# Attention of five of six head pairs in tied runs on TensorE

## Chip, cores and metric

The program runs on one core of one Trainium2 chip. The metric is the device time of one execution in microseconds, as a median over runs.

## What is computed

Two layers of a causal decoder, on a prompt of 1024 tokens and 8 single tokens with caches. The change lies in the prompt's attention. There are three groups of four heads of 64 channels; group g has window and dilation (128, 1), (512, 4), (2048, 16). A query reads the keys at distances 0, d, 2d, ... up to its window. The reference, cut to this:

```python
sc = jnp.einsum('brnqhd,brnkhd->brnhqk', qs, ks) * ATT_SCALE      # blocks of 128 queries, keys of the block before and its own
sc = jnp.where(mask[None, None, :, None], sc, NEG_INF)
m = jnp.max(sc, axis=-1, keepdims=True)
p = jnp.exp(sc - m)
l = jnp.sum(p, axis=-1, keepdims=True)
o = jnp.einsum('brnhqk,brnkhd->brnqhd', p, vs) / jnp.moveaxis(l, 3, 4)
...
att = jnp.sum(wts[..., None] * jnp.stack(outs, axis=0), axis=0)   # merge of the three groups
cv  = swish(layer_norm(causal_depthwise_conv31(a * sigmoid(gate))))
x   = x + concat(att, cv) @ w_o
x   = x + relu(rms_norm(x) @ w_up)**2 @ w_down
```

## The kernel before

Activations lie with channels on partitions, 1032 tokens along the free axis. All of it is fp32; the large products split both factors into a high and a low fp32r part and add three matmuls (lines 217 to 219, `ws_job`).

A layer's first half is a list of units, `STEPS` (line 60). `('g', j)` computes one 128-channel tile of the GLU (tile `gluL`) and sets off its convolution, 46 taps on VectorE (line 413). `('v', g)` and `('qk', g, p)` project v, and q and k of two heads, into `zv` and `zk`; then TensorE turns them by transposes (`tv`, `tz`, `tq`, `tk`). `('at', g, p)` is the attention of head pair p of group g, the function `attend`. `('ln',)` normalises the convolution's outputs, `('mg', p)` merges the groups for a head pair, and the products with w_o follow (`woL`).

`attend` works on eight tiles of 128 queries. A tile has one block of 128 keys (all of group 2, the even tiles of group 1, the first of group 0) or two. For two tiles at a time:
- scores, S: per tile and head one matmul (line 609) into the PSUM banks `sc`, one per head. Its operands have 64 rows, half of the array. The trace shows two matmul records for each fp32 matmul, so S of two tiles are eight.
- softmax: VectorE adds the mask and takes the extremum (line 618, into tile `sm`); ScalarE takes the exponential and its sum (line 621).
- turning, T: one transpose on TensorE per head and key block (line 628), into a bank `tr`, which ScalarE copies to `pT` (line 630). One record each.
- product with v, V: per head and key block one matmul (line 634) into the bank `pv`, with 64 columns of the array. Two records each: 4 per tile with one block, 8 with two.

In the program text T, the copy and V of the first tile precede T, the copy and V of the second; the next two tiles' S come after both. After four tiles ScalarE copies the bank `pv` to the output `O`.

There are two buffers each of `sc`, `tr`, `sm`, `pT`, one of `pv`, nine of `v` and three of `qT`. `sc` and `tr` are shared with the turnings of the q, k and v units.

Nothing in the program text fixes the order on an engine. A planner does it when the program is built: among the instructions whose inputs and buffers are ready by its own account of time it takes the one traced first (`later` and `next_piece` shift that place; the convolution's taps are traced 1300 places later). Each engine then runs its list strictly in that order. `tc.issue_after(ins)` adds one constraint: what is traced inside it comes behind `ins` in the list of the same engine; other instructions may still come in between.

So TensorE's list mixes large products of the units to come with the S, T and V of the attention at hand.

Of the kernel before, what the change touches and what calls it, by code (L numbers as in the profile page):

```python
# [7 lines left out]
F32 = mybir.dt.float32  # L8
F32R = mybir.dt.float32r
AF = mybir.ActivationFunctionType  # L10
ALU = mybir.AluOpType
# [4 lines left out]
P = 128  # L16
# [6 lines left out]
HD = 64  # L23
# [52 lines left out]
def tile_hybrid_decoder_step(  # L76
# [20 lines left out]
    nc = tc.nc  # L97
# [42 lines left out]
    def ps_s(name):  # L140
        return state["ps"].tile([P, 2, 256], F32, tag="sc", name=name, bufs=2)

    def ps_t(name):
        return state["ps"].tile([P, 4, P], F32, tag="tr", name=name, bufs=2)

    def ps_o(name):
        return state["ps"].tile([P, 4, P], F32, tag="pv", name=name, bufs=1)
# [74 lines left out]
    for l in range(DEPTH):  # L222
        for b in range(NB):
            for kv in range(2):
                for g, (win, _) in enumerate(GROUPS):
                    n = (win - 1) * 256
# [5 lines left out]
                    for q in range(parts):  # L232
                        o = q * rows * step
# [4 lines left out]
    def prow(l, what, j):  # L238
        base = {"mix": 0, "ffn": 8, "cb": 16, "lg": 22, "lb": 28}[what]
        return prm[:, NC_L * l + base + j:NC_L * l + base + j + 1]  # L240
# [4 lines left out]
    def act(k, name):  # L245

        return tp.tile([P, TOK], F32, tag="act", name=name, bufs=NCT) if k < NCT else big(name)

    def spare(name):

        return tp.tile([P, TOK], F32, tag="out", name=name, bufs=2)
# [93 lines left out]
    def by_group(t, g):  # L345

        if g == 0:
            return t
        if g == 1:
            return t.rearrange("p (i q) -> p q i", q=4)  # L350
        return t.rearrange("p (c r) -> p r c", r=16)

    def layer(l, x_dram, xin, last):
        nm = f"L{l}"
        xh, xl, rstd, norm_rest = xin
        with ExitStack() as pa:
            ap_ = pa.enter_context(tc.tile_pool(name=f"A{l}", bufs=1, reuse_waits="tile"))
# [17 lines left out]
            mask = ap_.tile([P, 256], F32, tag="mask", name=f"mask{nm}")  # L375
            mask2 = ap_.tile([P, P], F32, tag="mask2", name=f"mask2{nm}")
# [7 lines left out]
            vt = {}  # L384
            stat = {}
# [206 lines left out]
            def attend(g, p, qT, kT):  # L592
                if g not in stat:
                    stat[g] = ap_.tile([P, 8, 8], F32, tag="stat", name=f"stat{nm}_{g}", bufs=2)
                o_t = spare(f"O{nm}_{g}{p}")
                O = o_t[:, 0:SEQ]
                for half in range(2):
                    po = ps_o(f"po{nm}_{g}{p}{half}")
                    for n0 in range(4 * half, 4 * half + 4, 2):
                        tiles = []  # L600

                        sh = [ps_s(f"s{nm}_{g}{p}{n0}{h}") for h in range(2)]
                        for i in range(2):
                            n = n0 + i
                            blocks = (n - 1, n) if (g == 0 and n > 0) or (g == 1 and n % 2 == 1) else (n,)
                            tiles.append((n, blocks, P * len(blocks)))
                            for h in range(2):
                                hs = slice(HD * h, HD * h + HD)
                                nc.tensor.matmul(sh[h][:, i, :P * len(blocks)], qT[half][hs, n - 4 * half, :],  # L609
                                                 kT[hs, blocks[0]:n + 1, :].rearrange("p b t -> p (b t)"), start=True, stop=True)  # L610
                        sms = []
                        for i, (n, blocks, w) in enumerate(tiles):
                            sm = ap_.tile([P, 2, 256], F32, tag="sm", name=f"sm{nm}_{g}{p}{n}", bufs=2)
                            sms.append(sm)
                            mk = mask2 if g == 2 else (mask if len(blocks) == 2 else mask[:, P:256])
                            for h in range(2):
                                c = 2 * p + h
                                nc.vector.tensor_tensor_reduce(  # L618
                                    out=sm[:, h, :w], in0=sh[h][:, i, :w], in1=mk, scale=1.0, scalar=3.0e38,
                                    op0=ALU.add, op1=ALU.min, accum_out=stat[g][:, n, c:c + 1])  # L620
                                nc.scalar.activation(sm[:, h, :w], sm[:, h, :w], AF.Exp, bias=stat[g][:, n, c:c + 1], scale=-1.0,  # L621
                                                     accum_out=stat[g][:, n, 4 + c:5 + c])
                        for sm, (n, blocks, w) in zip(sms, tiles):
                            pt = ps_t(f"pt{nm}_{g}{p}{n}")
                            nbk = len(blocks)
                            for h in range(2):
                                for b in range(nbk):
                                    nc.tensor.transpose(pt[:, nbk * h + b, :], sm[:, h, P * b:P * b + P], ident)
                            pT = ap_.tile([P, 4, P], F32, tag="pT", name=f"pT{nm}_{g}{p}{n}", bufs=2)
                            nc.scalar.activation(pT[:, :2 * nbk, :], pt[:, :2 * nbk, :], AF.Copy)  # L630
                            for h in range(2):
                                for b in range(nbk):
                                    v = vt[g][blocks[b]]
                                    nc.tensor.matmul(po[HD * h:HD * h + HD, n - 4 * half, :],  # L634
                                                     v[:, P * p + HD * h:P * p + HD * h + HD],
                                                     pT[:, nbk * h + b, :], start=(b == 0), stop=(b == nbk - 1))
                    if g == 0:
                        nc.scalar.activation(O[:, 512 * half:512 * half + 512], po.rearrange("p n t -> p (n t)"), AF.Copy)
                    elif g == 1:
                        nc.scalar.activation(O.rearrange("p (b i q) -> p q b i", b=2, q=4)[:, 2 * half:2 * half + 2],  # L640
                                             po.rearrange("p (q b) i -> p q b i", q=2), AF.Copy)
                    else:
                        nc.scalar.activation(by_group(O, 2)[:, 8 * half:8 * half + 8],
                                             po.rearrange("p n (r c) -> p (n r) c", r=2), AF.Copy)
                if g > 0:
                    od = dp.tile([P, SEQ], F32, tag=f"od{g}{p}", name=f"od{nm}_{g}{p}", bufs=1)
                    nc.gpsimd.dma_start(od, O)
                    odram[g, p] = od
                else:
                    att[p] = o_t  # L650
# [170 lines left out]
            for what, *at in STEPS:  # L821
# [6 lines left out]
                elif what == "qk":  # L828
                    g, p = at
# [5 lines left out]
                elif what == "at":  # L835
                    g, p = at
# [8 lines left out]
                elif what == "sv":  # L845
                    values = sample_values(*sample_softmax())
# [56 lines left out]
        with ExitStack() as pb:  # L903
# [8 lines left out]
            def parts_of(op, name):  # L912

                out = []
                for i in range(2):
                    if op in ("t3", "b11", "t2", "t1", "b12"):
                        hl = [xs.tile([P, TOK], F32R, tag=t, name=f"{op}{t}{name}{i}", bufs=8) for t in ("xh", "xl")]
                    else:
                        hl = [bp.tile([P, TOK], F32R, tag=t, name=f"{op}{t}{name}{i}", bufs=6) for t in ("oh", "ol")]
                    out.append(tuple(t.rearrange("p (k t) -> p k t", k=2) for t in hl))  # L920
                return out
# [165 lines left out]
            o = ops["t2"] = parts_of("t2", f"U{nm}")  # L1087
# [97 lines left out]
            for g in range(1, NG):  # L1185
                c = {}
# [38 lines left out]
            for k in range(KD):  # L1225
                t = act(k, f"y{nm}_{k}")
                nc.scalar.dma_start(t, x_scr[:, k, :])
                y.append(t)
            for c in range(NG // 2):
                ops.clear()  # L1230
                for _, op in PRODUCTS:
                    o = ops[op] = parts_of(op, f"D{nm}_{c}")
                    for i in range(2):
                        h, lo_t = o[i]
# [137 lines left out]
    h, lo, acc, sq = norm_split(first, lambda k: prow(0, "mix", k), "m0", True)  # L1372

    ident = const.tile([P, P], F32, name="ident")
# [21 lines left out]
    for l in range(DEPTH):  # L1396
        src = (lambda k: xT[:, k, :]) if l == 0 else (lambda k: x_scr[:, k, :])
        last = Last(l)
# [105 lines left out]
```

## Time and profile before

| | |
|---|---|
| median of 3 runs | 2533.15 us (2531.63 to 2537.89) |
| profiled execution, its time | 2538.58 us |
| its span | 2536.8 us |
| mean granted clock of TensorE | 0.993 |
| instructions | 47393 |
| TensorE matmul, weight load | 2476.8 us (98%), 2337.9 us (92%) |
| VectorE, ScalarE, GpSimd | 1882.1 us (74%), 1081.1 us (43%), 240.3 us (9%) |

Busy time is the time in which an engine has at least one instruction in flight. TensorE's matmuls overlap, so the sum of their lengths is more than its busy time, and what a matmul costs is read from the distance of starts. An instruction's row has its line of the kernel, its output and inputs by the program's names, and its shape; for TensorE first the part of the array that it uses (128\*128 all of it, 64\*128 half of the rows, 128\*64 half of the columns). A row can stand for several instructions of one kind that follow each other.

### The profile page before, as it was taken

The numbers are of one execution on the slowest core, as the hardware profiler recorded it, in microseconds if no ns is written. First come the engines' busy times: TensorE is split into PE (matmuls) and PEld (weight loads), VectorE is DVE, ScalarE is ACT, GpSimd is POOL, SyncE is SP. The second block draws the span as 40 slices with busy tenths as digits, with TensorE's granted clock in tenths as the row PEclk, the third lists the DMA queues.
The fourth block names the chain that finished last, engine by engine and source line by source line (L and its number), as shares of the span: only waits on it lengthen the run. The fifth ranks groups of instructions, "written<-read, shape, count | busy, mean of one in ns | idle before, by whom it ended". The sixth has DMA issues, their size and how long they took to land. (4 is left out here: it accounts for less than half of the span.)

```text
span 2536.8 us, 47393 instructions
## 1 busy us (share of the span) xinstructions
PE 2476.8 (98%) x18872; PEld 2337.9 (92%) x18872; DVE 1882.1 (74%) x3308; ACT 1081.1 (43%) x2044; POOL 240.3 (9%) x445
## 2 busy tenths in 40 slices
PE   8999999998999999999999999999989999999997
PEld 7988988888999999999999888878989999999996
DVE  7988886677756687777778788766677756876776
ACT  5244447544433353334423443484444333543332
POOL 1001101011101021001010020010101101111000
PEclk9999999999999999999999999999999999999999
DMA  5324323353455587455333242243425555955451
GB/s 175 115 75 116 117 73 120 128 175 123 156 195 188 179 319 250 154 177 206 115 105 109 83 128 76 89 134 134 167 88 203 197 187 199 335 194 199 144 180 68
DMA packets 153390, 391.62 MB, mean 154 GB/s; under 512 B 32256, under 2 KB 54384, under 8 KB 150608
## 3 DMA queue, kind: packets, MB, share of 16 engines
q1 hardware_dynamic: 91072, 210.72, 25.5%
q0 software_dynamic: 43904, 147.95, 16.9%
q10 hardware_dynamic: 18192, 29.91, 3.5%
q8 instruction: 148, 2.42, 0.4%
q14 instruction: 74, 0.61, 0.1%
HBM read 299.38 MB, written 177.06 MB: 188 GB/s over the span
## 5 line engine op out<-in xcount | busy, mean ns | idle before, releaser
L217 PE MATMUL gluL<-xhm,whi 128*128 128x384 f32 (+2 forms) x592 | 188.6, 323 | 10.3 <-ACT whi L198 5.7
L219 PE MATMUL gluL<-xhm,wlo 128*128 128x384 f32 (+2 forms) x592 | 188.8, 321 | 0.0
L218 PE MATMUL gluL<-xlm,whi 128*128 128x384 f32 (+2 forms) x592 | 188.4, 320 | 0.4 <-DVE xlm L262 0.4
L217 PE MATMUL zkL<-xhm,whi 128*128 128x264 f32 (+2 forms) x576 | 187.4, 326 | 1.1 <-ACT zkL L476 1.1
L218 PE MATMUL zkL<-xlm,whi 128*128 128x256 f32 (+2 forms) x576 | 187.9, 326 | 0.0
L219 PE MATMUL zkL<-xhm,wlo 128*128 128x264 f32 (+2 forms) x576 | 186.5, 325 | 0.0
L199 DVE TENSOR_TENSOR wlo<-raw,whi 128x512 fp32r<-128x512 f32 x156 | 106.3, 687 | 40.9 <-ACT whi L198 39.0
L413 DVE SCALAR_TENSOR_TENSOR cL<-uL,cwt,cL 128x512 f32<-128x512 f32 x180 | 133.8, 743 | 0.3 <-ACT cL L411 0.3
L413 DVE SCALAR_TENSOR_TENSOR cL<-bxL,hsum,cL 128x512 f32<-128x512 f32 x180 | 133.8, 743 | 0.1
L198 ACT ACTIVATE whi<-raw 128x512 fp32r<-128x512 f32 x156 | 96.5, 632 | 82.2 <-DMA raw<-in_dram 44.9
L413 DVE SCALAR_TENSOR_TENSOR bxL<-uL,cwt,bxL 128x512 f32<-128x512 f32 x168 | 125.2, 745 | 0.0
L217 PEld LDWEIGHTS gluL<-xhm,whi 128*128 128x128 f32 x592 | 111.5, 189 | 13.3 <-ACT whi L198 5.7
L217 PEld LDWEIGHTS zkL<-xhm,whi 128*128 128x128 f32 x576 | 108.4, 188 | 13.1 <-issue 3.7
L219 PEld LDWEIGHTS zkL<-xhm,wlo 128*128 128x128 f32 x576 | 108.7, 189 | 12.8 <-issue 5.2
L218 PEld LDWEIGHTS zkL<-xlm,whi 128*128 128x128 f32 x576 | 108.5, 188 | 12.4 <-issue 4.9
L218 PEld LDWEIGHTS gluL<-xlm,whi 128*128 128x128 f32 x592 | 111.8, 189 | 2.2 <-DVE xlm L262 1.3
L219 PEld LDWEIGHTS gluL<-xhm,wlo 128*128 128x128 f32 x592 | 111.7, 189 | 2.1 <-issue 1.2
L1244 DVE TENSOR_TENSOR yL<-yL,paDL 128x516 f32<-128x516 f32 x128 | 87.3, 686 | 27.9 <-PE paDL L1156 27.9
L621 ACT ACTIVATE smL<-smL,statL 128x128 f32<-128x128 f32 (+1 forms) x192 | 84.6, 443 | 35.0 <-DVE statL L618 34.0
L217 PE MATMUL zvL<-xhm,whi 128*128 128x512 f32 (+2 forms) x288 | 95.5, 332 | 1.1 <-ACT zvL L473 0.8
L219 PE MATMUL zvL<-xhm,wlo 128*128 128x512 f32 (+2 forms) x288 | 93.2, 325 | 0.0
L218 PE MATMUL zvL<-xlm,whi 128*128 128x512 f32 (+2 forms) x288 | 93.0, 323 | 0.0
(525 smaller groups left out, 9235.2 us busy)
## 6 DMA issues: line engine op xcount, KB each, us to landing
raw<-in_dram SPq DMA_DIRECT2D x408, 256.0 KB
out_kvs_dram<-in_dram SPq DMA_DIRECT2D x128, 511.8 KB
out_kvs_dram<-in_dram SPq DMA_DIRECT2D x32, 511.0 KB
x_scr<-xL POOLq DMA_DIRECT2D x32, 258.0 KB, 3.5
fdL<-f11L POOLq DMA_DIRECT2D x16, 516.0 KB, 3.1
fdL<-f21L POOLq DMA_DIRECT2D x16, 516.0 KB, 5.0
fdL<-f22L POOLq DMA_DIRECT2D x16, 516.0 KB, 3.1
fdL<-t3fL POOLq DMA_DIRECT2D x16, 516.0 KB, 3.6
```

Of the source, the lines that this page charges most:

```text
L198: nc.scalar.activation(hi, raw, AF.Copy)
L199: nc.vector.tensor_tensor(lo, raw, hi.bitcast(F32), op=ALU.subtract)
L217: nc.tensor.matmul(out[:, :n], a, h, start=(k == 0), stop=False)
L218: nc.tensor.matmul(out[:, :n], a, l, start=False, stop=False)
L219: nc.tensor.matmul(out[:, :n], b, h, start=False, stop=(k == nk - 1))
L413: nc.vector.scalar_tensor_tensor(dst, src(m), tap(m), dst, op0=ALU.mult, op1=ALU.add)
L621: nc.scalar.activation(sm[:, h, :w], sm[:, h, :w], AF.Exp, bias=stat[g][:, n, c:c + 1], scale=-1.0, accum_out=stat[g][:, n, 4 + c:5 + c])
L1244: nc.vector.tensor_tensor(o, o, p, op=ALU.add)
```

## The change

`attend` is cut into four functions: `scores` (S and softmax of two tiles), `turn` (T of two tiles, last tile and last head first, and the copies to `pT`), `values` (V of two tiles) and `end` (the copy of the bank `pv`). The loop runs `turn` of the tiles at hand, then `values` of the two tiles before them, then `scores` of the next two. For all head pairs but (0, 1), TensorE's instructions are put behind one another by `issue_after`: the first T of a step stands behind the last S, every other T behind that first one, V behind the last T, the next S behind the last V. For (0, 1) there is no such tie, and `values` takes the tiles just turned.

```diff
+                po, last = {}, []
+                together = (g, p) != (0, 1)
+                def behind():
+                    return tc.issue_after(last[-1].ins) if last and together else nullcontext()
+                def scores(n0):
...
+                    with behind():
+                        for i in range(2):
...
+                                mm = nc.tensor.matmul(sh[h][:, i, :P * len(blocks)], qT[half][hs, n - 4 * half, :],
+                                                      kT[hs, blocks[0]:n + 1, :].rearrange("p b t -> p (b t)"), start=True, stop=True)
+                    last.append(mm)
...
+                def turn(tiles):
+                    pts = [ps_t(f"pt{nm}_{g}{p}{n}") for _, n, _ in tiles]
+                    for pt, (sm, n, blocks) in reversed(list(zip(pts, tiles))):
+                        nbk = len(blocks)
+                        for h in (1, 0):
+                            for b in range(nbk):
+                                with behind():
+                                    mm = nc.tensor.transpose(pt[:, nbk * h + b, :], sm[:, h, P * b:P * b + P], ident)
+                                if n == tiles[-1][1] and h == 1 and b == 0:
+                                    last.append(mm)
+                    last.append(mm)
...
+                def values(tiles):
+                    for pT, n, blocks in tiles:
+                        half, nbk = n // 4, len(blocks)
+                        if half not in po:
+                            po[half] = ps_o(f"po{nm}_{g}{p}{half}")
+                        for h in range(2):
+                            for b in range(nbk):
+                                v = vt[g][blocks[b]]
+                                with behind():
+                                    mm = nc.tensor.matmul(po[half][HD * h:HD * h + HD, n - 4 * half, :],
+                                                          v[:, P * p + HD * h:P * p + HD * h + HD],
+                                                          pT[:, nbk * h + b, :], start=(b == 0), stop=(b == nbk - 1))
+                    last.append(mm)
+                    n = tiles[-1][1]
+                    if n % 4 == 3:
+                        end(n // 4)
...
+                sm, pT = scores(0), None
+                for n0 in range(0, 8, 2):
+                    turned = turn(sm)
+                    if pT:
+                        values(pT)
+                    pT = turned
+                    if not together:
+                        values(pT)
+                        pT = None
+                    if n0 < 6:
+                        sm = scores(n0 + 2)
+                if pT:
+                    values(pT)
```

## Rows read from the trace of the kernel before

**Rows 1.** The page, engines: busy us, share of the span, instructions.

```profile
PE 2476.8 (98%) x18872; PEld 2337.9 (92%) x18872; DVE 1882.1 (74%) x3308; ACT 1081.1 (43%) x2044; POOL 240.3 (9%) x445
```

**Rows 2.** Stretches: length, busy PE, PEld, DVE, ACT, POOL, clock, DMA; layer 2's sum.

```profile
160.60:195.70 35.10, 35.10 (x236) 30.37 (x236) 21.47 (x65) 17.52 (x57) 0.22 (x2) 1.00 0.24 72
216.30:260.00 43.70, 40.99 (x294) 36.34 (x294) 37.31 (x90) 20.27 (x61) 9.82 (x15) 1.00 0.46 105
310.40:355.20 44.80, 44.80 (x286) 34.59 (x284) 39.86 (x86) 23.33 (x65) 1.49 (x2) 1.00 0.30 90
394.10:476.00 81.90, 81.90 (x597) 66.46 (x595) 49.95 (x137) 65.62 (x154) 10.14 (x18) 1.00 0.43 142
...
sum 206.40, PE 203.32 PEld 167.67 DVE 149.53 ACT 126.79 POOL 21.65; mean PE 50.83 PEld 41.92 DVE 37.38 ACT 31.70 POOL 5.41
```

**Rows 3.** Groups of instructions by shape, TensorE, 160.6 to 195.7 us.

```profile
L217 PE MATMUL gluL<-xhm,whi 128*128 128x384 f32 x32 | 11.1, 346 | 0.0
...
L217 PE MATMUL gluL<-xhm,whi 128*128 128x264 f32 x14 | 4.1, 289 | 0.0
```

**Rows 4.** Order of time, TensorE, around four V: start us, us, instruction.

```profile
175.32 0.28 PE L217 MATMUL gluL<-xhm,whi 128*128 128x264 f32 x1
175.53 0.44 PE L634 MATMUL poL<-pTL,vL 128*64 128x128 f32 x4
175.90 0.39 PE L218 MATMUL gluL<-xlm,whi 128*128 128x264 f32 x1
176.13 0.28 PE L219 MATMUL gluL<-xhm,wlo 128*128 128x264 f32 x1
```

**Rows 5.** Order of time, TensorE, around two T.

```profile
172.34 0.38 PE L628 MATMUL ptL<-ident,smL 128*128 128x128 f32 x2
172.47 0.37 PE L217 MATMUL gluL<-xhm,whi 128*128 128x264 f32 x1
172.68 0.28 PE L218 MATMUL gluL<-xlm,whi 128*128 128x264 f32 x1
172.80 0.28 PE L219 MATMUL gluL<-xhm,wlo 128*128 128x264 f32 x1
```

**Rows 6.** Order of time, TensorE, V, T and S in one run.

```profile
410.67 0.93 PE L634 MATMUL poL<-pTL,vL 128*64 128x128 f32 x12
411.53 0.44 PE L628 MATMUL ptL<-ident,smL 128*128 128x128 f32 x2
411.90 0.93 PE L609 MATMUL sL<-kTL,qTL 64*128 64x128 f32 x8
412.75 0.50 PE L218 MATMUL zkL<-xlm,whi 128*128 128x512 f32 x1
```

**Rows 7.** Order of time, TensorE, around eight S.

```profile
160.41 0.28 PE L219 MATMUL zkL<-xhm,wlo 128*128 128x264 f32 x1
160.62 0.72 PE L609 MATMUL sL<-kTL,qTL 64*128 64x128 f32 x8
161.27 0.44 PE L217 MATMUL gluL<-xhm,whi 128*128 128x384 f32 x1
161.55 0.33 PE L218 MATMUL gluL<-xlm,whi 128*128 128x384 f32 x1
161.72 0.34 PE L219 MATMUL gluL<-xhm,wlo 128*128 128x384 f32 x1
```

**Rows 8.** Order of time, first reduction and last exponential of two tiles.

```profile
220.49 0.29 DVE L618 CUSTOM_DVE_ANT_0 smL<-sL,mask2L 128x128 f32<-128x128 f32 x1
...
221.99 0.39 ACT L621 ACTIVATE smL<-smL,statL 128x128 f32<-128x128 f32 x1
```

**Rows 9.** Waits of TensorE, whole run: us in total, times, longest us.

```profile
PE poL L634 <- ACT pTL L630: 1.9, 2, 1.1
```

**Rows 10.** Waits of VectorE, 160 to 560 us.

```profile
DVE smL L618 <- PE sL L609: 12.3, 7, 6.1
```

**Rows 11.** Instructions on tile clL to 640 us: ns min/median/max, first and last start.

```profile
L860 DVE TENSOR_TENSOR clL<-cL,chL x6: 1217/1222/1231, 450.0 to 460.0; 128x1024 fp32r<-128x1024 f32 x6
```

More of the change, by code (lines that the diff above doesn't have):

```diff
@@ L596, in attend @@
                 O = o_t[:, 0:SEQ]
[L597 to L602, printed above, removed]
+                po, last = {}, []
[3 more added lines that the diff above has]
+                def scores(n0):
+                    half = n0 // 4
+                    tiles = []
+                    sh = [ps_s(f"s{nm}_{g}{p}{n0}{h}") for h in range(2)]
+                    with behind():
                         for i in range(2):
@@ L608, in attend @@
                                 hs = slice(HD * h, HD * h + HD)
[L609 to L636, printed above, removed]
+                                mm = nc.tensor.matmul(sh[h][:, i, :P * len(blocks)], qT[half][hs, n - 4 * half, :],
+                                                      kT[hs, blocks[0]:n + 1, :].rearrange("p b t -> p (b t)"), start=True, stop=True)
@@ new lines, in scores @@
+                    last.append(mm)
+                    out = []
+                    for i, (n, blocks, w) in enumerate(tiles):
+                        sm = ap_.tile([P, 2, 256], F32, tag="sm", name=f"sm{nm}_{g}{p}{n}", bufs=2)
+                        out.append((sm, n, blocks))
+                        mk = mask2 if g == 2 else (mask if len(blocks) == 2 else mask[:, P:256])
+                        for h in range(2):
+                            c = 2 * p + h
+                            nc.vector.tensor_tensor_reduce(
+                                out=sm[:, h, :w], in0=sh[h][:, i, :w], in1=mk, scale=1.0, scalar=3.0e38,
+                                op0=ALU.add, op1=ALU.min, accum_out=stat[g][:, n, c:c + 1])
+                            nc.scalar.activation(sm[:, h, :w], sm[:, h, :w], AF.Exp, bias=stat[g][:, n, c:c + 1], scale=-1.0,
+                                                 accum_out=stat[g][:, n, 4 + c:5 + c])
@@ new lines, in scores @@
+                    return out
+                def turn(tiles):
[9 more added lines that the diff above has]
+                    last.append(mm)
+                    out = []
+                    for pt, (sm, n, blocks) in reversed(list(zip(pts, tiles))):
+                        nbk = len(blocks)
+                        pT = ap_.tile([P, 4, P], F32, tag="pT", name=f"pT{nm}_{g}{p}{n}", bufs=2)
+                        out.append((pT, n, blocks))
+                        nc.scalar.activation(pT[:, :2 * nbk, :], pt[:, :2 * nbk, :], AF.Copy)
+                    return out[::-1]
@@ new lines, in values @@
+                def values(tiles):
[3 more added lines that the diff above has]
+                            po[half] = ps_o(f"po{nm}_{g}{p}{half}")
+                        for h in range(2):
+                            for b in range(nbk):
[8 more added lines that the diff above has]
+                        end(n // 4)
@@ L637, in attend, with end @@
+                def end(half):
+                    o = po[half]
                     if g == 0:
-                        nc.scalar.activation(O[:, 512 * half:512 * half + 512], po.rearrange("p n t -> p (n t)"), AF.Copy)
+                        nc.scalar.activation(O[:, 512 * half:512 * half + 512], o.rearrange("p n t -> p (n t)"), AF.Copy)
                     elif g == 1:
                         nc.scalar.activation(O.rearrange("p (b i q) -> p q b i", b=2, q=4)[:, 2 * half:2 * half + 2],
-                                             po.rearrange("p (q b) i -> p q b i", q=2), AF.Copy)
+                                             o.rearrange("p (q b) i -> p q b i", q=2), AF.Copy)
@@ L642, in attend @@
                     else:
                         nc.scalar.activation(by_group(O, 2)[:, 8 * half:8 * half + 8],
-                                             po.rearrange("p n (r c) -> p (n r) c", r=2), AF.Copy)
+                                             o.rearrange("p n (r c) -> p (n r) c", r=2), AF.Copy)
+                sm, pT = scores(0), None
[9 more added lines that the diff above has]
+                        sm = scores(n0 + 2)
```

## Prediction

> **What bounds the kernel now.** The table of engines comes first: TensorE has a matmul in flight for 2476.8 us of a span of 2536.8 us, VectorE is busy 74% and ScalarE 43% [rows 1]. So the time is TensorE's, and what counts is what a matmul occupies there, not how long its row says it lasts. Matmuls overlap: two rows of the 384-wide product start 0.17 us apart while each lasts 0.33 us [rows 7]. I therefore read all prices from start to start.
>
> The busy times of stretches come next. [...] The second layer's four sum to 206.4 us against 205.5 [rows 2], so one layer is worked out and doubled. Of each stretch I subtract all that is not attention, at its own pitch: a 384-wide product 0.175 us [rows 7], a 264- or 256-wide one 0.12 [rows 5], a 512-wide one 0.23 at the same rate per column, a turning for the next unit 0.11 [rows 5]. In the first stretch (group 2, pair 0) 32 and 14 products of line 217 [rows 3] stand for three times as many, since lines 217 to 219 take turns: 96 x 0.175 + 42 x 0.12 + 18 turnings x 0.11 = 23.8, which leaves 11.3 us for attention. The same subtraction from the same view gives 12.9 us for (2,1), with 96 products of 384, 91 of 264 or 256, one of 512 and 26 turnings; 16.6 for (1,0), with 61 of 512, 97 narrow ones and 24 turnings; and 29.4 for (1,1) with (0,0), with 72 of 512, 164 narrow ones, 51 of 384, 36 turnings and 3.3 us of norm sums. That is 70.2 us a layer.
>
> This is far more than the matmuls themselves need, and the order of time shows why. Four products with v (V) between 264-wide products: from the product at 175.32 to the second one after them is 0.81 us, of which two products are 0.24, so this visit costs 0.57 [rows 4]. Two turnings (T) cost 0.34 - 0.12 = 0.22, nothing beyond 0.11 each [rows 5]. Eight score matmuls (S) cost 0.85: 0.65 from the first to the next product, 0.09 more on the step in, 0.11 on the product after [rows 7]. In one unbroken run twelve V take 0.86 us and eight S, half of them 256 wide, 0.85 [rows 6]. With V4 at 0.37 [rows 4] a further V costs 0.06, so V8 is 0.61 and V16 1.10. A visit to V or S, which use half of the array's columns or rows, thus pays about 0.3 us for coming and going, whatever its length; a visit to T pays nothing.
>
> **The change part by part.** No instruction is added or removed; the order changes. In the five tied pairs all T of two tiles go first, behind the last exponential; then the V of the two tiles before; then the next S.
>
> Per two tiles of group 2, after: T4 0.44 + step from T to V 0.09 + V8 0.61 + S8 0.65 + slow product after 0.11 = 1.90 us. The step from V straight to S has no row. Its nearest rows are V's steps out, into a product [rows 4] and into T [rows 6], both contained in the 0.37 and 0.86 above and alike; and T2 between V and S, which takes 0.37 where two T are 0.22 [rows 6]. So a step into S costs between 0 and 0.15 beyond V8's own way out, 3 us over the 20 such steps of the kernel. I take 0, since S8's 0.65 already holds its slow second pair. [...]
>
> A head pair of eight tiles, four times two, becomes six visits: S alone, T S, twice T V S, T V, and V alone.
> - Group 2: 0.85 + (0.44 + 0.85) + 2 x 1.90 + (0.44 + 0.81) + 0.81 = 8.0 us.
> - Group 1 has T6, V12, and S8 half 256 wide (1.05 as a visit): 1.05 + 1.71 + 2 x 2.57 + 1.72 + 1.06 = 10.7. In (1,0) the first S8 falls into two visits now, outside what is tied: 11.7.
> - (0,0) has up to T8, V16, and S8 all 256 wide, estimated at 1.25 by adding 0.2 for each half: 2.1 + 1.91 + 2.99 + 3.23 + 2.18 + 1.30 = 13.7.
>
> Together 8.0 + 8.0 + 11.7 + 10.7 + 13.7 = 52.1 us against 70.2: 18.1 a layer, 36.2 in all. The stretch of (2,1) contains 2.7 us in which TensorE is idle [rows 2]; I count these as gone, since they are waits for a pTL copy, which V no longer follows at once, or stand behind it [rows 9]; if they stay, that is 5 us of the sum.
>
> Pair (0,1) stays untied, but its V of two tiles are now asked for together: between 0 and 4 x 0.32 us a layer. I take 0, since VectorE and ScalarE time its runs.
>
> The added wait: the first T of a run stands behind the last of four exponentials, and everything later on TensorE's queue stands behind that T, the products of the next unit included. Undisturbed, the four reductions and exponentials take 1.9 us, from 220.49 to 222.38 [rows 8]; with taps of the convolution (line 413) between them more. What hides them is the products that the order puts between S and T. If they are covered the price is 0, if none were it is 1.9 us for each of the 40 runs. VectorE now waits 12.3 us for S in this part of one layer [rows 10], so it has room before it is the late one. I take 0.1 us a run, 4 us. Scores are no longer issued ahead of T. That costs little: the `sm` tiles are two, both the current pair's, so the next reductions could not start before T in any case.
>
> The v tiles are held one step longer: nine slots, eight in use, so the next group's v turnings wait for the last V. I cost this at nothing: four steps of a 1.9 us run and a 1.9 us softmax with some taps in it are about 20 us, in stretches of 35 and more [rows 2]. If the last V came late nevertheless, TensorE would run out of the one GLU unit's products that stand beside (2,1). The DMA queues are not moved.
>
> Sum on the profiled execution: 2538.6 - 36.2 + 4 = 2506. The median of the runs shown is 5.4 us lower, so the forecast is **2501 us**.
>
> **Rivals.**
> 1. *The wait at the head of the run takes it back: slower than before.* Place: the first T of each run. It decides at 36.2 / 40 = 0.9 us per run. At 1.2 us the time is 2533 - 36 + 48 = 2545. For it: the softmax needs 1.9 us, more with taps between, and these stretches keep VectorE busy (37.3 of 43.7, 39.9 of 44.8 us) [rows 2]. Against: now VectorE waits for TensorE, not the other way; over the whole run V waits for a pTL copy twice, 1.9 us [rows 9].
> 2. *Half is lost.* The same waits at 0.5 us a run, 20 us, give 2517. It is the forecast's own weakness.
> 3. *VectorE's convolution chain does not come forward.* The w_o products need the split of the convolution's output, made between 450.0 and 461 us [rows 11]. If that stays where it is, TensorE runs out of products ahead of it and loses what was saved by then, some 15 of the 18 us: 2533 - 2 x 3 = 2527. Against: VectorE has 32 us of slack in the last stretch (49.9 of 81.9 busy) [rows 2], and the chain starts with GLU outputs that TensorE delivers earlier.
> 4. *The runs do not form*, since the order binds only TensorE's attention matmuls and lets products or the next unit's turnings (which share the S and T banks) in between. Then V of two tiles still merge in places: 10 to 15 visits of 0.3 us a layer, 2533 - 8 = 2525. Against: attention is traced ahead of the next unit and so goes first when both are ready.
> [...]
>
> **How the numbers follow.** No change from measurement is what lies within 0.3%, 7.6 us: 2525.5 to 2540.7. Chances: forecast 0.57, rival 2 0.18, rival 3 0.07, rival 4 0.08, rival 1 0.08, rival 5 0.02. Forecast and rival 2 are all but wholly faster, 3 and 4 stand at the edge and I split them, rival 1 is mostly slower: faster 0.80, within 0.3% 0.11, slower 0.09. The range goes down to 2488 (no waits, 4 us; pair (0,1), 2.6; the first S of (1,0) and (0,0) in one visit too, 4; and the rounding of some 90 visits), and up to 2530, which takes in rivals 2 to 4.
>
> **What would show it.** In the order of time of TensorE: T, V, S rows back to back, V rows of x8 and more, and fewer visits. Attention in the four stretches falls to 52 us a layer by the same subtraction. Idle before ptL stays under 0.3 us a run. The same gap at 1 us or more, or a hole before woL, would make the forecast wrong; as many V visits as now would say that the runs never formed.

## The result and the profile after

The changed kernel is slower: 2555.99 us (median of four runs, 2552.04 to 2558.25) against 2535.52 (2531.63 to 2538.34) on the same chip, a ratio of 1.008 with a 95% interval of 1.0059 to 1.0101. The forecast was 2501, the range 2488 to 2530. The profiled execution took 2552.04 us with a span of 2550.1, so the span grew by 13.3 us.

The table of engines, as in [rows 1]: TensorE is busy 17.3 us less in a span that is longer.

```profile
PE 2459.5 (96%) x18872; PEld 2350.0 (92%) x18872; DVE 1878.3 (74%) x3308; ACT 1075.0 (42%) x2044; POOL 239.6 (9%) x445
```

The four attention stretches of the first layer, each taken from its pair's first scores to its last copy, as in [rows 2]; the five tied pairs fill them. (2,0) takes 39.6 us for 35.1, (2,1) 49.3 for 43.7, (1,1) with (0,0) 91.0 for 81.9; only (1,0) is shorter, 42.4 for 44.8. The last stretch was full to the last microsecond and now contains 7.0 us of idle time, and the clock is no longer 1.00 in two of the four.

```profile
160.00:199.60 39.60, 39.60 (x283) 36.25 (x283) 31.76 (x82) 20.41 (x62) 1.72 (x4) 1.00 0.35 107
226.30:275.60 49.30, 46.45 (x320) 42.05 (x322) 45.65 (x106) 21.24 (x64) 10.06 (x15) 0.97 0.41 92
301.90:344.30 42.40, 42.40 (x312) 36.31 (x312) 38.73 (x84) 23.95 (x67) 1.48 (x2) 1.00 0.34 85
392.10:483.10 91.00, 84.00 (x632) 72.57 (x631) 46.25 (x132) 62.03 (x150) 9.42 (x16) 0.98 0.43 137
```

The order of time around one round of (0,0), as in [rows 6, 7]: T8, V12, S8 in one unbroken run. From the first T to the second product after the run it is 3.17 us; less one product of 0.175 that is 2.99, which is what the prediction computed for this run (it had bounded the step from V to S and taken it as 0; V12 takes 0.86 us up to S here, as it did up to T in [rows 6]).

```profile
458.25 0.33 PE L217 MATMUL woL<-chL,whi 128*128 128x384 f32 x1
458.42 1.03 PE L643 MATMUL ptL<-ident,smL 128*128 128x128 f32 x8
459.38 0.93 PE L664 MATMUL poL<-pTL,vL 128*64 128x128 f32 x12
460.24 1.13 PE L618 MATMUL sL<-kTL,qTL 64*128 64x256 f32 x8
461.31 0.45 PE L218 MATMUL woL<-clL,whi 128*128 128x384 f32 x1
461.59 0.34 PE L219 MATMUL woL<-chL,wlo 128*128 128x384 f32 x1
```

So the price of the run was right, and the loss is elsewhere. TensorE's waits in the first layer (160 to 620 us; total, times, longest) show where it lies. Before, there was no row for it between 425 and 560 us, and [rows 9] was all that its V waited; here the first, third and fourth row lie there.

```profile
PE ptL L643 <- ACT smL L631: 7.3, 3, 4.7
...
PE sL L618 <- ACT stL L577: 2.8, 1, 2.8
PE woL L218 <- DVE clL L912: 2.0, 2, 1.0
PE pwL L842 <- ACT wbL L839: 2.0, 2, 1.2
```

VectorE waits longer for scores too (160 to 560 us), 17.2 us against 12.3 [rows 10]:

```profile
DVE smL L628 <- PE sL L618: 17.2, 7, 5.8
```

The place where the half layer ends is the first w_l product (tile `wlL`, the last part of the products with w_o, in the next scope of PSUM banks; before and after, it starts right behind the last product of the merge, `pwL`). These are the stretches from 0 to that product, before, after, and in two experiments told below (all six pairs untied; order V S T): length, then busy PE.

```profile
0.00:551.70 551.70, 538.37 (x3582) 471.90 (x3583) 428.18 (x922) 264.55 (x605) 52.56 (x99) 0.99 0.38 115
```

```profile
0.00:558.00 558.00, 528.46 (x3583) 475.89 (x3583) 426.98 (x923) 261.90 (x606) 52.44 (x99) 0.98 0.38 116
```

```profile
0.00:542.40 542.40, 525.45 (x3581) 471.84 (x3582) 427.20 (x923) 261.97 (x606) 52.40 (x99) 0.99 0.39 119
```

```profile
0.00:539.80 539.80, 522.24 (x3582) 470.26 (x3583) 427.88 (x925) 262.46 (x606) 52.50 (x99) 0.99 0.39 120
```

Cut into windows of 10 us, with busy time x (1 - granted clock) as an estimate of the time that the lower clock level costs, they split as follows. The last column is what remains, by the same estimate TensorE's work at a clock of 1.00.

| us | first w_l product | idle | lower clock | work |
|---|---|---|---|---|
| before | 551.7 | 13.3 | 3.3 | 535.1 |
| after | 558.0 | 29.5 | 11.5 | 516.9 |
| no pair tied | 542.4 | 16.9 | 6.3 | 519.2 |
| order V S T | 539.8 | 17.6 | 5.3 | 516.9 |

The work fell by 18.2 us a layer; 18.1 were forecast. It was overpaid by 16.2 us of idle time and 8.2 of lower clock: +6.3 at the w_l product. The second layer repeats it: its first w_l product comes 14.6 us later than before (1817.8 against 1803.2), and the span ends 13.3 us later.

Where TensorE ran dry: the last w_o product starts at 550.0 us before and at 526.6 after (line 219, the last of the three; first and last start), the first w_l product at 551.7 and 558.0.

```profile
L219 PE MATMUL woL<-chL,wlo x108: 278/337/569, 456.0 to 550.0; 128*128 128x384 f32 x72, 128*128 128x264 f32 x36
```

```profile
L219 PE MATMUL woL<-chL,wlo x108: 278/336/525, 441.6 to 526.6; 128*128 128x384 f32 x72, 128*128 128x264 f32 x36
```

The w_o products are what fills the time beside the end of the attention. They now end 31 us ahead of w_l, and what is left beside the chain leaves a hole of 4.7 us. Behind the hole the clock is at 0.50: eight T of (0,1) take 1.97 us instead of the 1.03 above (the row), and the two stretches behind it are granted half.

```profile
538.24 1.97 PE L643 MATMUL ptL<-ident,smL 128*128 128x128 f32 x8 [4.66 <-ACT smL L631]
```

```profile
540.00:550.00 10.00, 8.00 (x41) 6.62 (x41) 5.12 (x13) 3.15 (x7) 0.00 (x0) 0.50 0.28 80
550.00:560.00 10.00, 9.94 (x46) 9.49 (x47) 5.28 (x10) 3.88 (x6) 0.00 (x0) 0.50 0.21 76
```

### The profile page after: what moved, and what is told of

The parts are those of the page before. It is cut to its first block, busy times and chain, and to the rows that moved or that the text cites. A ratio compares the mean times of both kernels' runs of the same rounds, so it can differ in the third digit from the quotient of the medians.

```text
span 2550.1 us, 47358 instructions
## 1 busy us (share of the span) xinstructions
PE 2459.5 (96%) x18872; PEld 2350.0 (92%) x18872; DVE 1878.3 (74%) x3308; ACT 1075.0 (42%) x2044; POOL 239.6 (9%) x445
## 3 DMA queue, kind: packets, MB, share of 16 engines
q0 software_dynamic: 43904, 147.95, 16.9%
## 5 line engine op out<-in xcount | busy, mean ns | idle before, releaser
L217 PE MATMUL zkL<-xhm,whi 128*128 128x256 f32 (+2 forms) x576 | 188.0, 327 | 1.9 <-ACT zkL L476 1.1
L631 ACT ACTIVATE smL<-smL,statL 128x128 f32<-128x128 f32 (+1 forms) x192 | 84.2, 441 | 41.6 <-DVE statL L628 41.4
```

The source lines that it names most:

```text
L217: nc.tensor.matmul(out[:, :n], a, h, start=(k == 0), stop=False)
```

## The experiments

All ratios are against the kernel before, on the same chip. S is the scores, T the turnings, V the products with v.

| kernel | us | ratio, 95% interval |
|---|---|---|
| ties in (2,0), (2,1), (1,0) alone | 2532.5 | 0.9997 (0.9987 to 1.0008) |
| ties in (1,1), (0,0) alone | 2546.8 | 1.0050 (1.0033 to 1.0066) |
| no ties, one-tile order | 2512.8 | 0.9916 (0.9901 to 0.9931) |
| no ties, V of the two tiles ahead | 2513.5 | 0.9921 (0.9907 to 0.9936) |
| ties without S | 2542.3 | 1.0033 (1.0023 to 1.0043) |
| S tied alone, behind V | 2513.9 | 0.9918 (0.9902 to 0.9935) |
| S tied alone, behind T | 2544.8 | 1.0044 (1.0030 to 1.0058) |
| order V S T, five pairs | 2507.5 | 0.9898 (0.9883 to 0.9913) |
| order V S T, six pairs | 2507.7 | 0.9889 (0.9874 to 0.9904) |
| after, more w_o products | 2563.8 | 1.0121 (1.0100 to 1.0143) |
| before, more w_o products | 2572.9 | 1.0147 (1.0126 to 1.0167) |
| order V S T, more w_o products | 2535.2 | 1.0003 (0.9993 to 1.0012) |

### Which pairs

The first theory came from the traces: the late pairs (1,1) and (0,0) are a serial chain, and two-tile rounds lengthen it.

```diff
-                together = (g, p) != (0, 1)
+                together = (g, p) in ((2, 0), (2, 1), (1, 0))
```

> Ties only in the pairs (2,0), (2,1) and (1,0), whose rounds have w products waiting beside them; (1,1), (0,0) and (0,1) go one tile at a time as before. Theory (the end of the first half of each layer is one serial chain, softmax of (1,1) and (0,0), second projection, attention (0,1), closing of the PSUM scope; the two-tile rounds of (1,1) and (0,0) lengthen it and leave TensorE without work): the early pairs keep their saving, the first w_l product comes at 545 to 550 us instead of 558, and the time is 2510 to 2525 us. Rival (ties hold TensorE back wherever they are): 2540 us or more. Rival (the lower clock between 510 and 580 us is itself the loss, and comes with the runs of turnings): some of it stays, 2530 to 2545 us.

```diff
-                together = (g, p) != (0, 1)
+                together = (g, p) in ((1, 1), (0, 0))
```

> Ties only in the pairs (1,1) and (0,0); the others go one tile at a time as before. Theory (the serial end of the first half of each layer is lengthened by the two-tile rounds of these pairs): slower than before, 2545 to 2565 us, with the last w_o product earlier than the first w_l product by 15 us or more. Rival (ties hold TensorE back wherever they are, three of five pairs being untied here): 2538 to 2545 us. Rival (the clock falls because of the runs in all pairs): about 2540 us.

```diff
-                together = (g, p) != (0, 1)
+                together = False
```

> No pair is tied: the changed kernel's code with the one-tile order in all six pairs. Theory: the time of the kernel before, 2530 to 2545 us, since nothing but the order of the five pairs differs between the two. Rival (something else in the rewritten code, such as where the tiles of v are held, costs the time): 2548 to 2560 us.

The early ties alone missed the theory's time (2532.5 us for 2510 to 2525), the late ones met it (2546.8). The last is the surprise. With no tie at all the rewritten code takes 2512.8 us, 0.84% less than before; the theory said "the time of the kernel before" and was wrong in that. What is left of the change there is an order: the T of both tiles are asked for ahead of the V of both (and the second tile's T first), where before each tile's V followed its own T. The two were not tried apart. The planner then merges the visits by itself. The table above gives 15.9 us less work a layer for it, 87% of what the ties reach.

Against that kernel (differences of the ratios, times 2533 us) the ties cost 20 us in the three early pairs, 34 in the two late ones, 42 in all five. So the late pairs pay most, as the theory said, but the early ones pay too, as its rival said. (Such a difference of two ratios is good to about 5 us by their intervals.)

### Two tiles ahead, without ties

```diff
-                    return tc.issue_after(last[-1].ins) if last and together else nullcontext()
+                    return nullcontext()
```

> Two tiles at a time with the products with v of the two tiles ahead, as in the changed kernel, but without the ties: each instruction goes where the order by costs and due times puts it. Theory (the latency of a two-tile round, not the tie, lengthens the chain): 2545 to 2560 us, with the first w_l product again 4 us or more later than before. Rival (the tie is what holds the round: next scores wait for the head of the run): faster, 2515 to 2535 us.

2513.5 us: the tie is what costs, and asking for V two tiles later is worth nothing by itself. My theory had the latency of the two-tile round as the cause, and fell.

### Which tie

Each run of the changed kernel has two edges between kinds that nothing in the data asks for: V of the two tiles before stands behind T, and the next S behind that V. The next runs take them one at a time. A third tie, of every other T behind the first, stays in the run without S; it stays in the order V S T below too, and costs nothing there.

```diff
-                    with behind():
+                    with nullcontext():
                         for i in range(2):
                             n = n0 + i
```

> The changed kernel with the scores taken out of the ties; turnings and products with v stay tied, in all five pairs. Theory (revised after the first four runs: the turnings and products merge into long visits without any tie, and what the ties cost is that the next scores wait behind the turnings and the products with v, so that the next reductions start 2 to 3 us later in each round): the loss goes, 2510 to 2520 us, with rounds of (0,0) of about 6 us from turning to turning as without ties, against 8.5 us. Rival (the head of the run, that is turnings and products tied together, holds TensorE's other work back): 2540 us or more, rounds still over 8 us.

2542.3 us: V behind T without the tie of S costs 30 us against the kernel with no pair tied (28 against the one with V of the two tiles ahead), so the theory that the place of S is all of it fell.

```diff
-                                with behind():
+                                with nullcontext():
                                     mm = nc.tensor.transpose(...)
...
-                                with behind():
+                                with nullcontext():
                                     mm = nc.tensor.matmul(po[half]...)
```

> The changed kernel with only the scores tied (behind the turnings and the products with v that precede them); turnings and products with v are free. Theory (the scores' tie alone is the loss): 2545 to 2560 us, as slow as the changed kernel, rounds of (0,0) of 8 us or more. Rival (the head of the run is the loss): 2510 to 2525 us.

2513.9 us, no loss. But this was not the test that I meant: V, now free, goes ahead of T (V12 at 402.0, T6 at 404.6 us), and S, tied to that V alone, went ahead of T with it. It shows that S behind V is free. It shows one thing more: the first step of a pair has no V yet, so its S was tied to T, and in all ten such rounds it followed T ((1,1): last T at 396.99, S at 397.19 us) without any loss in the time. So the edge from T to S costs nothing in the first round of a pair by itself. In the other rounds it needed its own kernel: the same, with

```diff
                     last.append(mm)
                     n = tiles[-1][1]
...
-                    last.append(mm)
```

in `values`, so that S is tied to the T before it.

> The changed kernel with one tie left: the next scores stand behind the turnings of the two tiles before them; turnings and products with v are free. (In the run with scores tied behind the products with v alone, those products went ahead of the turnings, and the scores with them, so that this edge was not tested there.) Theory (the place of the next work behind the turnings, that is behind the last exponential, is what lengthens a round; products with v behind the turnings cost some 29 us by the run with free scores, scores the rest): 2522 to 2535 us, rounds of (0,0) of 7 us or more. Rival (only the two edges together cost): 2510 to 2518 us, rounds of about 6 us.

2544.8 us: 32 us for this edge alone (31 against the kernel with V of the two tiles ahead), more than either theory said. The two edges cost 30 and 32 us alone and 42 together; both are work placed behind T.

Starts of T (order of time, TensorE) from the end of (1,1) on show the rounds. With no pair tied:

```profile
437.87 0.81 PE L643 MATMUL ptL<-ident,smL 128*128 128x128 f32 x6
...
449.06 1.03 PE L643 MATMUL ptL<-ident,smL 128*128 128x128 f32 x8
...
454.84 1.04 PE L643 MATMUL ptL<-ident,smL 128*128 128x128 f32 x8
...
460.79 1.04 PE L643 MATMUL ptL<-ident,smL 128*128 128x128 f32 x8
```

After, where (0,0) starts 14 us later and a third T8, at 475.9, ends it:

```profile
451.53 0.82 PE L643 MATMUL ptL<-ident,smL 128*128 128x128 f32 x6
...
458.42 1.03 PE L643 MATMUL ptL<-ident,smL 128*128 128x128 f32 x8
...
467.01 1.03 PE L643 MATMUL ptL<-ident,smL 128*128 128x128 f32 x8
```

Ties without S, and S behind T alone:

```profile
448.03 1.09 PE L643 MATMUL ptL<-ident,smL 128*128 128x128 f32 x8 [0.52 <-ACT smL L631]
...
455.53 1.03 PE L643 MATMUL ptL<-ident,smL 128*128 128x128 f32 x8
...
463.36 1.04 PE L643 MATMUL ptL<-ident,smL 128*128 128x128 f32 x8
```

```profile
461.29 1.04 PE L643 MATMUL ptL<-ident,smL 128*128 128x128 f32 x8
...
468.20 1.04 PE L643 MATMUL ptL<-ident,smL 128*128 128x128 f32 x8
...
474.67 1.04 PE L643 MATMUL ptL<-ident,smL 128*128 128x128 f32 x8
```

From T8 to T8 it is 5.8 and 6.0 us untied, 8.6 and 8.9 after, 7.5 and 7.8 with V behind T, 6.9 and 6.5 with S behind T. In this last kernel more of the loss lies ahead of (0,0), whose first T6 starts at 454.4 us: VectorE waits 21.4 us for scores between 390 and 485 us, against 8.8 untied.

```profile
DVE smL L628 <- PE sL L618: 21.4, 6, 6.2
```

The longer rounds of (0,0) are the sign of the edges, but most of the time is not lost there. From the first T6 to the last T8 (0,0) takes 22.9 us untied, 24.4 after, 24.8 with V behind T and 20.3 with S behind T. The first layer by milestones, each against the kernel with no pair tied:

| us later than with no pair tied | first T of (1,1) | its fourth T6 | last T8 of (0,0) | first S of (0,1) | first w_l product |
|---|---|---|---|---|---|
| after | 3.3 | 15.5 | 15.1 | 15.0 | 15.6 |
| ties in (1,1), (0,0) alone | -0.6 | 13.1 | 15.4 | 15.3 | 16.0 |
| S tied alone, behind T | 5.8 | 17.3 | 13.9 | 12.0 | 17.3 |
| ties without S | 0.0 | 3.2 | 2.6 | 5.1 | 10.4 |

After, and with S behind T alone, most of the loss arises within (1,1). There other work comes between: in its last round after, the exponentials start 4.6 us after the first reduction (430.68 and 426.06 us), behind ScalarE's pass over the convolution's outputs (line 869); untied 0.3 us after it (413.50 and 413.17), and that pass comes later. With V behind T and S free, three quarters of it arise behind the last T8 of (0,0), most of that in the first softmax of the untied pair (0,1). How much of the loss each of these makes was not tried.

### The order V S T

If T is where the round waits, the ties are harmless as long as T comes last.

```diff
                 for n0 in range(0, 8, 2):
-                    turned = turn(sm)
-                    if pT:
-                        values(pT)
-                    pT = turned
...
+                    if together:
+                        if pT:
+                            values(pT)
+                        ahead = scores(n0 + 2) if n0 < 6 else None
+                        pT = turn(sm)
+                        sm = softmax(*ahead) if ahead else None
...
```

(`softmax` is the reductions and exponentials, split off from `scores`.)

> The five pairs tied as in the changed kernel, but the run is in the order products with v, next scores, turnings: the next scores stand ahead of the turnings, so that the reductions can start as soon as the turnings have freed the tiles. Theory (the loss is the scores' place behind the turnings, not the tie): 2508 to 2520 us, rounds of (0,0) of about 6 us. Rival (any tie through all three kinds holds TensorE back): 2535 us or more.

2507.5 us, the fastest kernel here beside the next one, with T8 at 445.8, 451.6 and 457.7 us. One round of it, all engines (order of time; the last row is the last exponential):

```profile
451.61 1.03 PE L646 MATMUL ptL<-ident,smL 128*128 128x128 f32 x8
...
452.36 0.42 DVE L631 CUSTOM_DVE_ANT_0 smL<-sL,maskL 128x256 f32<-128x256 f32 x1 [3.46 <-PE ptL L646]
...
454.76 0.50 ACT L634 ACTIVATE smL<-smL,statL 128x256 f32<-128x256 f32 x1
```

And the same in the changed kernel, whose T, V and S of this round stand in the result:

```profile
461.51 0.43 DVE L628 CUSTOM_DVE_ANT_0 smL<-sL,maskL 128x256 f32<-128x256 f32 x1 [3.16 <-PE sL L618]
...
463.48 0.49 ACT L631 ACTIVATE smL<-smL,statL 128x256 f32<-128x256 f32 x1
```

The first reduction starts 0.75 us after the first T in the one, waiting for T, and 3.09 us after it in the other, waiting for S. That is 2.3 us in this round, and the reductions wait for the last thing in the run. Over the 30 such steps from one round to the next in the five pairs and both layers, the median is 0.8 us in the order V S T, 1.1 with no pair tied, 2.2 with S behind T alone and 3.1 after. The last exponential of the round starts 3.15 and 5.06 us after the first T.

The edge from T to V works on another engine. V frees the two `pT` tiles into which T is copied next; with V behind T the copies are late and fall between the exponentials. ScalarE in the kernel with ties without S, the four exponentials of one round (L631) with two copies of T (L652) and one of the output between them:

```profile
456.74 0.51 ACT L631 ACTIVATE smL<-smL,statL 128x256 f32<-128x256 f32 x1 [4.16 <-DVE statL L628]
...
457.74 0.58 ACT L652 ACTIVATE pTL<-ptL 128x512 f32<-128x512 f32 x1
458.21 0.50 ACT L631 ACTIVATE smL<-smL,statL 128x256 f32<-128x256 f32 x1
...
458.71 0.58 ACT L652 ACTIVATE pTL<-ptL 128x512 f32<-128x512 f32 x1
459.19 0.59 ACT L675 ACTIVATE OL<-poL 128x512 f32<-128x512 f32 x1
459.66 0.51 ACT L631 ACTIVATE smL<-smL,statL 128x256 f32<-128x256 f32 x1
```

With no pair tied, both copies are done first and the four follow one another:

```profile
455.54 1.09 ACT L652 ACTIVATE pTL<-ptL 128x512 f32<-128x512 f32 x2 [2.27 <-PE ptL L643]
456.51 0.51 ACT L631 ACTIVATE smL<-smL,statL 128x256 f32<-128x256 f32 x1
...
457.99 0.50 ACT L631 ACTIVATE smL<-smL,statL 128x256 f32<-128x256 f32 x1
```

From first T to the start of the last exponential that is 4.1 us (from 455.53) against 3.2 (from 454.84). TensorE's V is what the copies wait for there between 390 and 485 us (no such wait in the untied kernel):

```profile
ACT pTL L652 <- PE poL L664: 3.8, 2, 3.0
```

So V behind T costs 28 to 30 us by the run; that it costs them by these late copies is argued from the trace and not shown. Four `pT` tiles would test it.

> Products with v, next scores, turnings in this order in all six pairs, (0,1) too. Theory (the serial stretch from (0,1)'s first scores to the first w_l product sets the end of the half layer; in this order its rounds are no longer than without ties, since scores still stand ahead of the turnings): 2503 to 2512 us, no more than 4 us from the kernel with five pairs in this order. Rival (a tie in the pair without enough other products costs again): 2515 us or more.

The same code with `together = True`: 2507.7 us, no different. A tie in the pair with the fewest products beside it costs nothing in this order.

### Is TensorE out of work, and what is the clock

```diff
             ws_job(p, pieces, P * f, ch[2:], cl[2:], lo, w)
+            if un == 0:
+                ws_job(p, pieces, P * f, ch[2:], cl[2:], lo, w)
```

> The changed kernel with a part of the w_o products done twice (about 0.17 us each, some 17 us a layer, 34 us in all), behind the attention of the last pairs. Theory (TensorE has run out of products there and waits for the serial chain, and its clock is at the lower level in that stretch): most of the added work lies in the hole, 2550 to 2570 us, with the granted clock higher than 0.50 between 540 and 560 us. Rival (TensorE is the bound there too, and the products only moved): 2585 to 2595 us.

> The kernel before with the same 216 w_o products done twice as in the changed kernel's run with more filler. Theory (before the change TensorE has products up to the first w_l product, so that added ones show in full: 216 times 0.175 us is 38 us): 2562 to 2575 us. Rival (there is slack there in the kernel before as well): 2545 us or less.

> Five pairs in the order products with v, scores, turnings, with the same 216 w_o products done twice. Theory (this kernel too runs out of products before the first w_l product, by 4 us of idle and about 5 us of lower clock in each layer): 2518 to 2532 us, 11 to 25 us more than without the added products, of their 38. Rival (nothing is idle there any more): 2542 to 2548 us.

The 216 products are 144 of 384 columns and 72 of 264, so 34 us, not 38. By the ratios they cost 37 us before, all of their price: there is no slack. After, they cost 10, so some 24 us of TensorE's time lay unused in the two layers together. In the order V S T they cost 27, a little more than expected (11 to 25): some 7 us are still unused there.

In the changed kernel with these products the clock is 1.00 through the stretch where it was 0.50:

```profile
540.00:550.00 10.00, 8.85 (x82) 8.05 (x82) 6.92 (x26) 5.15 (x14) 0.64 (x1) 1.00 0.20 52
550.00:560.00 10.00, 10.00 (x73) 9.84 (x73) 5.87 (x11) 3.87 (x6) 0.00 (x0) 1.00 0.01 2
```

So the low clock went with the lack of w_o products there (0.50 without the added ones, 1.00 with them), not with the runs: those at 458 to 470 us of the changed kernel go at 1.00. By the table it is a part of the price (8 of the 24 us a layer that were lost), and by this run a consequence.

## Why the prediction was wrong

**What bounds the kernel: right, but read one step too short.** TensorE bounds the kernel before; the added products in it cost their full price. But it was full because w_o products lasted until 1.7 us ahead of w_l. The work taken away beside the serial chain was gained only until the filler ended (last w_o product at 526.6 us after, first w_l product at 558.0), and the prediction asked what is late next only for single waits, not for the whole chain of (1,1), (0,0), second projection of (0,1), attention (0,1) and w_l. Even without ties 3.6 us of idle and 3.0 of lower clock a layer come back this way.

**The price of a visit: right. The 18.1 us a layer: nearly, with some luck.** T8 V12 S8 took the 2.99 us that were computed, and the step from V to S, bounded by 0 and 0.15 us and taken as 0, is not above 0 in that run. The prediction's subtraction, made for the four stretches after the change (an estimate: busy time x granted clock, less the other products at the same pitches), leaves 7.7, 8.1, 10.9 and 25.7 us of attention: 52.4 us where 52.1 were forecast. But 2.7 of the 18.1 us were idle time in (2,1) that was counted as gone, and (2,1) has 2.85 us of it after. The forecast of work alone was 15.4 us, and these stretches gave 15.1 of it (70.2 - 2.7 - 52.4); the table's 18.2 reaches up to the w_l product and takes in the untied pair (0,1), whose merged V were put at nothing.

**That the ties bring it: wrong.** 15.9 of the 18.2 come from asking for T T V V instead of T V T V.

**The step that failed:** "Scores are no longer issued ahead of T. That costs little: the `sm` tiles are two, both the current pair's, so the next reductions could not start before T in any case." They could not start before T, but with scores ready they start 0.75 us after the first T, and with scores behind T and V 3.09 us after it. Before, the next scores stood ahead of the first T in 12 of the 30 rounds and between the first T and the last in the other 18; after, behind the last T in all. The tie of S behind T alone costs 32 us where the forecast had nothing. The same blindness holds for V: the prediction followed the held v tiles, and not the `pT` tiles that V frees; the tie of V behind T, without S, costs 30 us.

**The wait at the head of the run, 0.1 us each: right as a wait of TensorE.** Of the 7.3 us for which T waits in the first layer, 4.9 lie in the untied pair (0,1); the 20 tied runs have 2.4, that is 0.12 us each. Rival 1 had the sign and came nearest in time (2545 us), but put the price on the first T's wait. In the order V S T that T still stands behind all four exponentials, and nothing is lost (2507.5 us). What costs is what is put behind T, not that T waits.

**Rivals 3 and 4, and the clock.** w_o starts 14.4 us earlier (441.2 against 455.6), so VectorE's chain did come forward; the wait for `clL` is 2.0 us. The runs formed. The clock fell, but where it did at a run, idle time stood ahead: in the second layer two runs of (1,1), with T at 1670.95 and 1691.02 us, have a clock of 0.67 and 0.66 in the 5 us from T on, which is some 3.4 us at 0.50 (an estimate from these), behind 1.80 and 2.35 us of idle time. Turnings stand at both clocks in this trace: between 538 and 558 us TensorE does turnings, one-column products and V, is 80 to 99% busy, and stays at 0.50; the runs of (0,0) between wide products at 458 to 470 us go at 1.00.

## What to carry to other kernels

When a run on one engine is tied together, look at each instruction behind the one that waits longest: what it feeds or frees on the other engines starts later (here the next reductions 3.09 us after the first T instead of 0.75). Put what is ready ahead of it, and the waiting instruction last. And ask for work in the order that merges visits before forcing that order: here the plain request gave seven eighths of the saved work and about a quarter of the loss (6.6 of 24.4 us a layer).

## What was not expected of the hardware

A hole of 4.7 us is followed by some 20 us at the lower clock although TensorE is busy again at once (80% and 99% of the two 10 us windows): 0.50 from 538 to 560 us, and 0.92 from 560 to 570 us, the w_l products having begun at 558.0. In the untied kernel 3.9 us of idle time are followed by 0.50 from 530 to 540 us, with TensorE busy for 9.98 of the 10. So in the changed kernel more is lost behind the hole than in it: 4.7 us of idle time, and behind it 8.5 of the 11.5 us that the lower clock costs in the first layer.

The hole is not needed for it, though. In the kernel before TensorE has no idle time from 530 to 552 us, and the clock falls there too, among turnings, one-column products and the last 264-wide w_o products:

```profile
540.00:550.00 10.00, 10.00 (x74) 9.96 (x73) 5.90 (x10) 5.15 (x8) 0.00 (x0) 0.91 0.24 79
550.00:552.00 2.00, 2.00 (x13) 1.92 (x12) 2.00 (x5) 1.15 (x2) 0.00 (x0) 0.60 0.00 0
```

What these three cases share is turnings and one-column products just ahead of the low stretch or in it; whether the idle time or these bring it was not separated.
